# A decoder block's last loop: a weight tile loaded earlier, a residual read before the end, and 56 blocks of u spread over 128 turns

## The chip, the cores and the metric

One core of a Trainium2 chip runs the whole kernel. The metric is device time in microseconds (us); lower is better. TensorE (PE) multiplies matrices, VectorE (DVE) and ScalarE (ACT) work elementwise, GpSimd (POOL) issues the indirect loads, and SyncE (SP) issues the other loads and stores. Each engine works through its instructions in a fixed order and waits at the first one whose inputs are not there.

## What is computed

The reference is one decoder layer on 512 tokens of width 1024. Two token mixers (a gated recurrence and a dilated window attention) come first, then a channel mixer that retrieves experts:

```
x = x + merged @ w_out
h2 = rms_norm(x)
x = x + peer_ffn(h2, peer_wq, peer_subkeys, peer_u, peer_v)

# peer_ffn: 16384 experts (128 x 128 keys), 8 heads, the best 16 of each head
hid = einsum('thkd,td->thk', u[ib], xb)
a   = gelu(hid) * gate
out = einsum('thk,thkd->td', a, v[ib])
```

All is float32. The change is in the last part, the product with v.

## The kernel before

The 512 tokens are four tiles of 128. For three of the tiles (`VD`) the kernel does not gather rows of v: it goes through all 16384 experts in 128 blocks of 128 and multiplies densely, with weights that are zero where a token did not choose an expert. For the fourth tile (T = 3) it gathers the chosen rows one index at a time; the first product is dense for two tiles and gathered for the other two.

Before the last loop, 72 blocks of u (`NPRE`) are multiplied with the tokens: `hidden(b)` (L794 to L812) loads one 512 KB block `ub` through SP (L804), and PE writes `ph` (L811), of which ScalarE makes `pre[b]` (L812). Each token's expert weights are meanwhile scattered into a table `g_d` in device memory (L704).

The last loop (L844 to L867) makes 128 turns, one block of v each:

- Every eighth turn (`GB` = 8) the next eight blocks' weights are loaded from `g_d` into `Gc` through SP (L849), 1536 KB. Two buffers take turns, in the pools `vs` and `dp`. The eight blocks of group 0 are already on chip.
- VectorE multiplies block b's weights with `pre[b]` in place (L852), and the result is split into a high and a low part, `ah` by ScalarE and `al` by VectorE (L853, in the helper at L96 and L97).
- SP loads the block of v, `vb` (L855, 512 KB, three buffers), and ScalarE and VectorE split it into `vh` (L857) and `vl` (L859), two buffers each.
- PE adds 18 products to six accumulators, two for each of the three tiles (L863): `ah` with `vh`, `ah` with `vl`, `al` with `vh`. The accumulators stay in PSUM for the whole loop.
- In the first 56 turns `hidden(b + 72)` (L866) makes the remaining blocks of u, here with both operands split (`uh`, `ul`, one buffer each; 24 products). Its result is stored where `pre[b]` lay.
- `rows(ROWS_D)` (L867) emits the gathered rows of tile 3: GpSimd loads 128 rows of u or v by index (L636) into one of four buffers (three `rowx`, one `row`), and VectorE multiplies or accumulates them (L648, L667). A `Pump` (class at L708) pays out 1.9 of them a turn. A row's load also waits for that turn's `vh` (L640).

Behind the loop the rest of the rows is emitted (L868), and each of the three tiles is finished (L869 to L875): the residual, which an earlier part wrote to the output, is read back into the one buffer `row`, the two accumulators are added, and the tile is written.

The order in which the code emits the instructions is only a priority. A planner simulates the engines and queues when the kernel is built, and sets each engine's order by what is ready then in the simulation. So a step may run some turns after the turn that emits it.

Of the kernel before, what the change touches and what calls it, by code (L numbers as in the profile page):

```python
# [8 lines left out]
F32 = mybir.dt.float32  # L9
# [9 lines left out]
P = 128  # L19
S = 512  # L20
D = 1024
# [6 lines left out]
NKEY = 128  # L28
# [13 lines left out]
VD = (1, 2, 0)  # L42
NU = len(UD) * P
GT = 16
NGT = len(VD) * P // GT
GB = 8
# [5 lines left out]
NPRE, RING = 72, 56  # L52
# [3 lines left out]
GS = 4  # L56
ACTW = (4, 12)

ROWS_H, ROWS_D = 0.6, 1.9
UBUFS = 3  # L60
UK, WBUFS, WSBUFS, ATB = 4, 2, 4, 2

# [9 lines left out]
def kernel(ctx: ExitStack, tc: tile.TileContext, x, wst, par, cst, cols, g2, keys, u, v, ut, vr, out):  # L72
    nc = tc.nc
# [21 lines left out]
    def halves(hi, lo, x, eng=None):  # L95
        nc.scalar.activation(hi, x, AF.Copy)  # L96
        (eng or nc.vector).tensor_tensor(out=lo, in0=x, in1=hi.bitcast(F32), op=ALU.subtract)  # L97
        return hi, lo

    def accumulate(out, ws, xs, cut, w_stays, k0=0, last=KC - 1):  # L100

        for k, w in enumerate(ws, k0):
            if isinstance(w, tuple):
                x = xs[0][:, k], xs[1][:, k]
                ops = [(w[0], x[0]), (w[0], x[1]), (w[1], x[0])]
            else:
                ops = [(w, xs[:, k])]
            for i, (w, x) in enumerate(ops):
                l, r = (w[:, cut], x) if w_stays else (x[:, cut], w)
                nc.tensor.matmul(out, l, r, start=(k == 0 and i == 0), stop=(k == last and i == len(ops) - 1))  # L110
# [565 lines left out]
    g_d = dram.tile([P, NGT, NKEY, GT], F32, name="g_d")  # L676
# [52 lines left out]
    rows, scat = Pump(), Pump()  # L729
# [29 lines left out]
    gat = ctx.enter_context(tc.tile_pool(name="gat", bufs=1, side="left", **TILE))  # L759
# [26 lines left out]
    dp = ctx.enter_context(tc.tile_pool(name="dp", bufs=1, side="right", **TILE))  # L786
    rx = ctx.enter_context(tc.tile_pool(name="rx", bufs=3, side="right", **TILE))
    us = ctx.enter_context(tc.tile_pool(name="us", bufs=UBUFS, side="right", **TILE))
    row_places[:] = [(rx, "rowx")] * 3 + [(gat, "row")]
    pre, pre4 = [], [None]  # L790

    Gcs = [dp.tile([P, NGT, GB, GT], F32, name="Gc")]

    def hidden(b, pool):  # L794
        if RING <= b < NPRE:

            if (b - RING) % 4 == 0:
                pre4[0] = rq_pool.tile([P, 4, NU], F32, name="rq") if b - RING < 12 else rq_pool.tile([P, 4, NU], F32, name="keys_sb", bufs=1)
            dst = pre4[0][:, (b - RING) % 4]
        else:  # L800
            dst = dp.tile([P, NU], F32, name="pre", bufs=RING)
        pre.append(dst)
        ub = us.tile([P, KC, P], F32, name="ub")
        nc.sync.dma_start(out=ub, in_=ut[b].rearrange("p (k i) -> p k i", k=KC))  # L804
        pt = pool.tile([P, NU], F32, name="ph")
        if b < NPRE:

            accumulate(pt, [ub[:, k] for k in range(KC)], h32, slice(None), True)
        else:
            ubs = halves(us.tile([P, KC, P], F32R, name="uh", bufs=1), us.tile([P, KC, P], F32R, name="ul", bufs=1), ub)  # L810
            accumulate(pt, [tuple(a[:, k] for a in ubs) for k in range(KC)], (hH, hL), slice(None), True)  # L811
        return nc.scalar.activation(dst, pt, AF.Gelu)  # L812
# [26 lines left out]
    ph = ctx.enter_context(tc.tile_pool(name="ph", bufs=1, space=PSUM, side="left", **TILE))  # L839
    vs = ctx.enter_context(tc.tile_pool(name="vs", bufs=2, side="left", **TILE))  # L840
    pacc = ctx.enter_context(tc.tile_pool(name="pacc", bufs=1, space=PSUM, side="right", **TILE))
    ngu = NU // GT
    acc = [[pacc.tile([P, 512], F32, name=f"acc{t}{c}") for c in range(2)] for t in range(len(VD))]
    for b in range(NKEY):  # L844
        if b % GB == 0:
            Gc = Gcs[0]
            if b:
                Gc = (vs if b // GB % 2 else dp).tile([P, NGT, GB, GT], F32, name="Gc", bufs=1)
                nc.sync.dma_start(out=Gc, in_=g_d[:, :, b:b + GB])  # L849
        a = pre[b]  # L850
        gsl = Gc[:, :, b % GB]
        nc.vector.tensor_mul(gsl[:, :ngu], a.rearrange("p (g t) -> p g t", t=GT), gsl[:, :ngu])  # L852
        aH, aL = halves(vs.tile([P, NGT, GT], F32R, name="ah"), vs.tile([P, NGT, GT], F32R, name="al"), gsl)  # L853
        vb = vs.tile([P, D], F32, name="vb", bufs=3)
        nc.sync.dma_start(out=vb, in_=vr[b])  # L855
        vH = vs.tile([P, D], F32R, name="vh")
        behind[:] = [nc.scalar.activation(vH, vb, AF.Copy)]  # L857
        vL = vs.tile([P, D], F32R, name="vl")
        nc.vector.tensor_tensor(out=vL, in0=vb, in1=vH.bitcast(F32), op=ALU.subtract)  # L859
        for t in range(len(VD)):  # L860
            for i, (l, r) in enumerate([(aH, vH), (aH, vL), (aL, vH)]):
                for c in range(2):
                    nc.tensor.matmul(acc[t][c], l.rearrange("p g t -> p (g t)")[:, t * P:(t + 1) * P], r[:, c * 512:(c + 1) * 512],  # L863
                                     start=(b == 0 and i == 0), stop=(b == NKEY - 1 and i == 2))
        if b + NPRE < NKEY:
            hidden(b + NPRE, ph)  # L866
        rows(ROWS_D)  # L867
    rows(2 * S)  # L868
    for t, T in enumerate(VD):  # L869
        x1r = gat.tile([P, D], F32, name="row")  # L870
        nc.sync.dma_start(out=x1r, in_=out[T * P:(T + 1) * P])
        for c in range(2):
            cs = slice(c * 512, (c + 1) * 512)
            nc.vector.tensor_add(x1r[:, cs], acc[t][c], x1r[:, cs])
        nc.sync.dma_start(out=out[T * P:(T + 1) * P], in_=x1r)  # L875


def layout(inputs):
# [36 lines left out]
def build(arrays):  # L915
    import concourse.bacc as bacc
    nc = bacc.Bacc("TRN2", target_bir_lowering=False, num_devices=1)
    args = {k: nc.dram_tensor(f"in_{k}_dram", a.shape, mybir.dt.from_np(a.dtype), kind="ExternalInput").ap()
            for k, a in arrays.items()}
    out = nc.dram_tensor("out_0_dram", (S, D), F32, kind="ExternalOutput").ap()  # L920
    with tile.TileContext(nc, schedule_with_timeline_sim=True) as tc:
        kernel(tc, **args, out=out)
    return nc
# [8 lines left out]
```

## Time and profile before

| | us |
|---|---|
| median of three timed runs | 1810.34 (1808.81 to 1812.05) |
| the profiled execution, its own time | 1805.38 |
| its span in the trace | 1803.5 |
| start of the last loop's products in the span | 1059.3 |
| end of the last product | 1785.1 |

The rows below come from that one execution. A row of the timeline starts with the start in us from the span's start and the duration in us, then the engine, the line, the operation, what is written from what, and how many instructions are merged; in square brackets stands how long the engine was idle ahead of it and what ended that. "SPq" is SyncE's queue of issues. A row of a window gives the stretch, its length, each engine's busy time with its instructions, the clock that was granted to TensorE as a share of full speed, the busy share of the DMA engines and the GB/s moved. A row of the waits names who waited for whom, the total in us, how often, and the longest.

### The profile page before, as it was taken

The page shows a single profiled execution, that of the slowest core. Times are in us where ns is not written, and L with a number is a line of the kernel's source. Part 1 is how long each engine was busy: PE and PEld are TensorE (multiplying, and loading weights), DVE is VectorE, ACT ScalarE, POOL GpSimd, SP SyncE. Part 2 cuts the span into 40 slices and gives each one's busy share as a digit, 9 for nine tenths or more (in the row PEclk, how much of TensorE's full clock was granted, in tenths as well). Part 3 has the DMA queues.
Part 4 walks back from the last instruction along what each step waited for, and adds up shares of the span by engine and source line. Part 5 has one row for each costly group of instructions (what it writes and reads, how often), then busy time and mean ns, then how long its engine had stood idle before and what let it go on. Part 6 is the DMA issues. An engine that isn't in the chain of part 4 may idle for free.

```text
span 1803.5 us, 26810 instructions
## 1 busy us (share of the span) xinstructions
PE 1639.0 (91%) x9725; PEld 1450.2 (80%) x9725; DVE 1346.3 (75%) x2805; ACT 700.8 (39%) x1283; POOL 641.5 (36%) x502
## 2 busy tenths in 40 slices
PE   8998979789988799999899889999999999988995
PEld 7887968689877797888789877888888888867774
DVE  3113999989886669998985577787788887777774
ACT  3323434334344544523454553334344333323331
POOL 0000355766550004452442123334444444443330
PEclk9999979999989899999999999999999999989998
DMA  8776468788884336665667688999999998888885
GB/s 287 245 232 221 143 206 312 245 296 306 304 287 170 119 121 240 208 201 193 211 227 252 225 293 308 331 355 333 331 335 342 331 331 315 286 281 300 299 293 183
DMA packets 173380, 473.41 MB, mean 262 GB/s; under 512 B 14784, under 2 KB 62144, under 8 KB 173248
## 3 DMA queue, kind: packets, MB, share of 16 engines
q1 hardware_dynamic: 115840, 268.47, 43.9%
q0 software_dynamic: 55296, 201.35, 31.3%
q10 hardware_dynamic: 2112, 1.88, 0.3%
q8 instruction: 77, 1.26, 0.3%
q14 instruction: 55, 0.45, 0.1%
HBM read 442.80 MB, written 27.79 MB: 261 GB/s over the span
## 4 chain that ended last, share of the span: by engine, by line
PE 47%; DVE 25%; DMA 21%; issue 4%; ACT 2%; POOL 1%; DVEq 0%; POOLq 0%; ACTq 0%; SPq 0%
PE acc L863 18%; PE pp L110 16%; DMA Gc<-g_d 9%; PE ph L110 9%; DMA w<-in_wst_dram 2%; DMA rq<-in_u_dram,idx 2%; DVE e L687 2%; DVE rowx L648 2%; PE pg L701 2%; DMA rowx<-in_u_dram,idx 2%; DVE rq L648 1%; DVE row L648 1%; DVE eg L696 1%; DMA row<-in_u_dram,idx 1%; DVE wl L97 1%
## 5 line engine op out<-in xcount | busy, mean ns | idle before, releaser
L110 PE MATMUL ph<-h,ub 128*128 128x256 f32 x1152 | 265.4, 386 | 0.0
L863 PE MATMUL acc<-vl,ah 128*128 128x512 f32 x768 | 243.5, 398 | 18.0 <-DVE vl L859 18.0
L863 PE MATMUL acc<-vh,al 128*128 128x512 f32 x768 | 244.3, 396 | 0.0
L110 PEld LDWEIGHTS ph<-h,ub 128*128 128x128 f32 x1152 | 219.2, 195 | 29.8 <-issue 0.2
L863 PE MATMUL acc<-vh,ah 128*128 128x512 f32 x768 | 221.1, 396 | 9.8 <-ACT vh L857 9.8
L636 POOL DMA_INDIRECT rowx<-in_u_dram,idx x96 | 122.7, 1278 | 216.1 <-ACT pre L812 56.8
L636 POOL DMA_INDIRECT rowx<-in_v_dram,idx x96 | 130.7, 1362 | 193.2 <-DVE h2g L667 90.2
L863 PEld LDWEIGHTS acc<-vl,ah 128*128 128x128 f32 x768 | 145.2, 192 | 49.3 <-DVE vl L859 20.8
L863 PEld LDWEIGHTS acc<-vh,ah 128*128 128x128 f32 x768 | 143.9, 191 | 38.8 <-ACT vh L857 11.1
L863 PEld LDWEIGHTS acc<-vh,al 128*128 128x128 f32 x768 | 146.5, 192 | 30.5
L96 ACT ACTIVATE ah<-Gc 128x384 fp32r<-128x384 f32 x128 | 67.0, 524 | 264.0 <-PE acc L863 261.3
L859 DVE TENSOR_TENSOR vl<-vb,vh 128x1024 fp32r<-128x1024 f32 x128 | 156.1, 1219 | 11.6 <-ACT vh L857 11.2
L857 ACT ACTIVATE vh<-vb 128x1024 fp32r<-128x1024 f32 x128 | 135.6, 1060 | 45.3 <-DMA vb<-in_vr_dram 44.5
L636 POOL DMA_INDIRECT rq<-in_u_dram,idx x96 | 120.0, 1250 | 93.5 <-DVE rq L648 52.9
L648 DVE SCALAR_TENSOR_TENSOR rowx<-rowx,h2g 128x1024 f32<-128x1024 f32 x96 | 122.4, 1276 | 39.2 <-DMA rowx<-in_u_dram,idx 39.1
L648 DVE SCALAR_TENSOR_TENSOR rq<-rq,h2g 128x1024 f32<-128x1024 f32 x96 | 132.8, 1385 | 19.8 <-DMA rq<-in_u_dram,idx 19.6
L96 ACT ACTIVATE wh<-w 128x512 fp32r<-128x512 f32 x144 | 89.1, 629 | 128.8 <-PE pp L110 71.1
L110 PE MATMUL ph<-hH,ul 128*128 128x256 f32 x448 | 127.6, 285 | 5.1 <-DVE ul L97 5.1
L110 PE MATMUL ph<-hH,uh 128*128 128x256 f32 x448 | 127.8, 285 | 3.8 <-ACT pre L812 3.8
L667 DVE SCALAR_TENSOR_TENSOR h2g<-rowx,hid,h2g 128x1024 f32<-128x1024 f32 x95 | 121.7, 1281 | 8.4 <-DMA rowx<-in_v_dram,idx 8.0
L110 PE MATMUL ph<-hL,uh 128*128 128x256 f32 x448 | 127.7, 285 | 0.0
L701 PE MATMUL pg<-eg,e 128*128 128x128 f32 x768 | 104.5, 290 | 23.5 <-DVE eg L696 17.3
(289 smaller groups left out, 3611.9 us busy)
## 6 DMA issues: line engine op xcount, KB each, us to landing
ub<-in_ut_dram SPq DMA_DIRECT2D x128, 512.0 KB, 4.7
vb<-in_vr_dram SPq DMA_DIRECT2D x128, 512.0 KB, 7.1
w<-in_wst_dram SPq DMA_DIRECT2D x107, 512.0 KB, 5.2
g_d<-Gx SPq DMA_DIRECT2D x24, 960.0 KB, 4.6
Gc<-g_d SPq DMA_DIRECT2D x15, 1536.0 KB, 16.5
wh<-in_wst_dram SPq DMA_DIRECT2D x37, 256.0 KB, 4.9
wl<-in_wst_dram SPq DMA_DIRECT2D x33, 256.0 KB, 5.4
pairB<-in_x_dram SPq DMA_DIRECT2D x5, 512.0 KB
```

The lines of the kernel that those rows point to most:

```text
L96: nc.scalar.activation(hi, x, AF.Copy)
L97: (eng or nc.vector).tensor_tensor(out=lo, in0=x, in1=hi.bitcast(F32), op=ALU.subtract)
L110: nc.tensor.matmul(out, l, r, start=(k == 0 and i == 0), stop=(k == last and i == len(ops) - 1))
L636: d = nc.gpsimd.indirect_dma_start(out=r, out_offset=None, in_=src, in_offset=bass.IndirectOffsetOnAxis(ap=index, axis=0))
L648: nc.vector.scalar_tensor_tensor(r, r, 1.0, h2g[T], op0=ALU.mult, op1=ALU.mult, accum_out=hid[:, g, j:j + 1])
L667: nc.vector.scalar_tensor_tensor(acc, r, hid[:, g, j:j + 1], acc, op0=ALU.mult, op1=ALU.add)
L687: nc.vector.tensor_tensor(out=e1, in0=iota[:, None, :, 0].to_broadcast(by_token), in1=pk[:, ti, 0, tk, None].to_broadcast(by_token), op=AL ...
L696: nc.vector.tensor_tensor(out=eg, in0=e2.rearrange("p k q -> p q k"), in1=pkw[:, ti, tk, None].to_broadcast(by_token), op=ALU.mult)
L701: nc.tensor.matmul(pt[:, q], e1[:, q0 + q], eg[:, q0 + q], start=True, stop=True)
L857: behind[:] = [nc.scalar.activation(vH, vb, AF.Copy)]
L859: nc.vector.tensor_tensor(out=vL, in0=vb, in1=vH.bitcast(F32), op=ALU.subtract)
L863: nc.tensor.matmul(acc[t][c], l.rearrange("p g t -> p (g t)")[:, t * P:(t + 1) * P], r[:, c * 512:(c + 1) * 512], start=(b == 0 and i == 0 ...
```

## The change

- The weights `Gc` of group g + 1 are loaded in the middle of group g (turn 8g + 4), into the same two buffers.
- The 56 remaining blocks of u are emitted one in every 2.14 turns, the last by turn 118 (`ULAST` = 120), in place of one a turn in the first 56 turns.
- The gathered rows are emitted at 1.75 a turn in place of 1.9; what might be left is emitted in turn 123 (`XLAST`) and no longer behind the loop.
- In turn 123 the three tiles' residuals are read into the three `rowx` buffers. Behind the loop only the adds and the writes are left, and each tile is written in two halves.

```diff
--- before.py
+++ after.py
@@ -56,7 +56,9 @@
 GS = 4
 ACTW = (4, 12)
 
-ROWS_H, ROWS_D = 0.6, 1.9
+ROWS_H, ROWS_D = 0.6, 1.75
+
+ULAST, XLAST = 120, 123
 UBUFS = 3
 UK, WBUFS, WSBUFS, ATB = 4, 2, 4, 2
 
@@ -842,11 +844,12 @@
     ngu = NU // GT
     acc = [[pacc.tile([P, 512], F32, name=f"acc{t}{c}") for c in range(2)] for t in range(len(VD))]
     for b in range(NKEY):
-        if b % GB == 0:
-            Gc = Gcs[0]
-            if b:
-                Gc = (vs if b // GB % 2 else dp).tile([P, NGT, GB, GT], F32, name="Gc", bufs=1)
-                nc.sync.dma_start(out=Gc, in_=g_d[:, :, b:b + GB])
+        if b % GB == GB // 2 and b + GB < NKEY:
+
+            g = b // GB + 1
+            Gcs.append((vs if g % 2 else dp).tile([P, NGT, GB, GT], F32, name="Gc", bufs=1))
+            nc.sync.dma_start(out=Gcs[g], in_=g_d[:, :, g * GB:(g + 1) * GB])
+        Gc = Gcs[b // GB]
         a = pre[b]
         gsl = Gc[:, :, b % GB]
         nc.vector.tensor_mul(gsl[:, :ngu], a.rearrange("p (g t) -> p g t", t=GT), gsl[:, :ngu])
@@ -862,17 +865,22 @@
                 for c in range(2):
                     nc.tensor.matmul(acc[t][c], l.rearrange("p g t -> p (g t)")[:, t * P:(t + 1) * P], r[:, c * 512:(c + 1) * 512],
                                      start=(b == 0 and i == 0), stop=(b == NKEY - 1 and i == 2))
-        if b + NPRE < NKEY:
-            hidden(b + NPRE, ph)
+
+        if len(pre) < NKEY and (len(pre) - NPRE) * ULAST <= b * (NKEY - NPRE):
+            hidden(len(pre), ph)
         rows(ROWS_D)
-    rows(2 * S)
+        if b == XLAST:
+
+            rows(2 * S)
+            x1s = []
+            for T in VD:
+                x1s.append(rx.tile([P, D], F32, name="rowx"))
+                nc.sync.dma_start(out=x1s[-1], in_=out[T * P:(T + 1) * P])
     for t, T in enumerate(VD):
-        x1r = gat.tile([P, D], F32, name="row")
-        nc.sync.dma_start(out=x1r, in_=out[T * P:(T + 1) * P])
         for c in range(2):
             cs = slice(c * 512, (c + 1) * 512)
-            nc.vector.tensor_add(x1r[:, cs], acc[t][c], x1r[:, cs])
-        nc.sync.dma_start(out=out[T * P:(T + 1) * P], in_=x1r)
+            nc.vector.tensor_add(x1s[t][:, cs], acc[t][c], x1s[t][:, cs])
+            nc.sync.dma_start(out=out[T * P:(T + 1) * P, cs], in_=x1s[t][:, cs])
 
 
 def layout(inputs):
```

## Rows read from the trace of the kernel before

**Rows 1.** The page, part 1: busy us (share of the span) x instructions, by engine.
```profile
PE 1639.0 (91%) x9725; PEld 1450.2 (80%) x9725; DVE 1346.3 (75%) x2805; ACT 700.8 (39%) x1283; POOL 641.5 (36%) x502
```

**Rows 2.** Windows: length, busy of PE, PEld, DVE, ACT, POOL, clock, DMA, GB/s.
```profile
1059.32:1580.54 521.22, 510.40 (x2822) 443.94 (x2821) 414.24 (x551) 200.07 (x279) 215.15 (x155) 0.99 0.92 327
1580.54:1785.08 204.54, 182.89 (x758) 147.86 (x756) 153.07 (x175) 60.96 (x81) 71.57 (x55) 0.93 0.81 282
...
1360.00:1485.00 125.00, 125.00 (x699) 109.30 (x699) 104.94 (x112) 50.01 (x70) 55.50 (x40) 1.00 0.95 337
```

**Rows 3.** Waits of PE in the loop: total us, times, longest us.
```profile
PE acc L863 <- DVE vl L859: 18.0, 6, 8.2
PE acc L863 <- ACT vh L857: 9.8, 3, 4.0
PE ph L110 <- DVE ul L97: 4.6, 5, 2.5
```

**Rows 4.** Timeline of PE: two turns' starts; a block of u, start and next.
```profile
1768.60 1.52 PE L863 MATMUL acc<-vh,ah 128*128 128x512 f32 x6
...
1772.68 1.52 PE L863 MATMUL acc<-vh,ah 128*128 128x512 f32 x6
...
1577.70 0.28 PE L110 MATMUL ph<-hH,uh 128*128 128x256 f32 x1
...
1580.54 0.63 PE L863 MATMUL acc<-vh,ah 128*128 128x512 f32 x2
```

**Rows 5.** Timeline of SP's queue: loads behind the cut.
```profile
1580.69 0.53 SPq L849 DMA_DIRECT2D Gc<-g_d  x1
1581.83 41.44 SPq L855 DMA_DIRECT2D vb<-in_vr_dram  x8
...
1706.59 61.48 SPq L855 DMA_DIRECT2D vb<-in_vr_dram  x14
```

**Rows 6.** Timeline, all engines: waits at Gc loads behind the cut.
```profile
1596.93 2.77 DVE L852 TENSOR_TENSOR Gc<-pre,Gc 128x256 f32<-128x256 f32 x8 [8.87 <-DMA Gc<-g_d]
1598.26 1.06 ACT L857 ACTIVATE vh<-vb 128x1024 fp32r<-128x1024 f32 x1 [5.17 <-DMA vb<-in_vr_dram]
...
1602.55 1.22 PE L863 MATMUL acc<-vl,ah 128*128 128x512 f32 x2 [8.20 <-DVE vl L859]
...
1643.49 1.66 PE L863 MATMUL acc<-vh,ah 128*128 128x512 f32 x6 [2.53 <-ACT vh L857]
...
1722.71 1.06 ACT L857 ACTIVATE vh<-vb 128x1024 fp32r<-128x1024 f32 x1 [6.16 <-DMA vb<-in_vr_dram]
...
1723.82 2.38 PE L863 MATMUL acc<-vh,ah 128*128 128x512 f32 x6 [3.29 <-ACT vh L857]
```

**Rows 7.** Waits of ScalarE, 1059 to 1585 us, then 1585 to 1785 us.
```profile
ACT vh L857 <- DMA vb<-in_vr_dram: 20.1, 9, 4.1
...
ACT vh L857 <- DMA vb<-in_vr_dram: 23.6, 4, 6.9
```

**Rows 8.** Timeline behind the last product: SP's issues and VectorE's adds.
```profile
1787.26 0.33 SPq L871 DMA_DIRECT2D row<-out_dram  x1
1790.94 1.29 DVE L874 TENSOR_TENSOR row<-acc,row 128x512 f32<-128x512 f32 x2 [6.34 <-DMA row<-out_dram]
...
1798.42 1.29 DVE L874 TENSOR_TENSOR row<-acc,row 128x512 f32<-128x512 f32 x2 [6.19 <-DMA row<-out_dram]
1799.73 0.34 SPq L875 DMA_DIRECT2D out_dram<-row  x1
```

**Rows 9.** Row loads, L636: POOL in windows; then forms, ns, first and last start.
```profile
1050.00:1785.00 735.00, 289.57 (x212) 0.97 0.89 315
1360.00:1485.00 125.00, 55.50 (x40) 1.00 0.95 337
...
L636 POOL DMA_INDIRECT rowx<-in_u_dram,idx x63: 933/1307/1999, 1055.9 to 1330.0; - x63
L636 POOL DMA_INDIRECT row<-in_v_dram,idx x32: 932/1336/2855, 1342.0 to 1763.3; - x32
...
DMA to landing us min/median/max: 4.8/7.6/13.7
```

## The prediction

> **What bounds the kernel now.** I read the page first: TensorE (PE) is busy 91% of the span, VectorE 75% [rows 1]. A share that high hides where the rest is lost, so next I cut the last loop of 128 turns at the place where the last u block is through. The loop's first product stands at 1059.3 us, its last ends at 1785.1. Up to 1580.5 PE is busy 510.4 of 521.2 us at a granted clock of 0.99 with the DMA engines at 0.92; after that 182.9 of 204.5 us at 0.93, DMA at 0.81 [rows 2]. The same loop is tight while u blocks run beside the v blocks, and loose once they are used up.
>
> How many turns lie behind the cut: after the Gc load at 1580.69 SP issues four runs of vb loads, of 8, 8, 8 and 14 (the first and the last are shown) [rows 5], 38 in all, so the first of them is block 90; three blocks are held ahead, and the turn that starts at 1580.54 is number 86. Thus 86 turns and all 56 u blocks lie before the cut and 42 turns behind it.
>
> What they need when nothing is late: turns follow each other every 4.08 us (1768.60, 1772.68), and a u block takes PE from 1577.70 to 1580.54, 2.84 us [rows 4]. Before the cut 86 x 4.08 + 56 x 2.84 = 509.9 us are needed and 521.2 taken: 11.3 lost, 2.2%. Behind it 42 x 4.08 = 171.4 are needed and 204.5 taken: 33.2 lost, 8.3 for each of the four Gc loads there. The whole loop needs 681.3 us and takes 725.8, so 44.5 us are to be had, three quarters of it in the last third. PE's own list of waits puts 32.4 us on three lines: 18.0 on vl, 9.8 on vh, 4.6 on ul [rows 3]; the other 12 are products at the lower clock behind the gaps (a granted clock of 0.93 behind the cut is 2.4 GHz for most of the time and 1.2 for the rest).
>
> Why it waits is seen at one load. Gc is issued at 1580.69 [rows 5]. VectorE stands 8.87 us until it lands, then multiplies eight blocks; only behind these, on the same in-order engine, comes vl, and PE stands 8.20 us. The vb load issued right behind Gc, at 1581.83, is late too: ScalarE waits 5.17 us for it [rows 6]. So each boundary has two causes, Gc in front of VectorE and Gc in front of a vb.
>
> **The tail.** After the last product three tiles are finished one after the other through one buffer: read back (1787.26), add (1790.94), write, read back, add (1798.42), last write issued at 1799.73 [rows 8]. From 1785.1 to the span's end are 18.4 us, with nothing on PE. The chain is 1059.3 + 725.8 + 18.4 = 1803.5; 1.9 us lie outside the span, own time 1805.4. The median of the three timed runs is 1810.3, 4.9 above; I work on the own time and add 4.9 at the end.
>
> **The change, part by part.** *Tail.* The three reads move to turn 123, into the three rowx buffers, so nothing is read back after the sums. Each accumulator is added as soon as it is ready. The last turn's products go tile by tile, 6 x 0.227 = 1.36 us each, and two adds take 1.29 [rows 8], so two tiles' adds lie beside PE and one pair is left. Then the last issue and what followed it: 1803.5 - 1799.73 = 3.8. New tail 0.2 + 1.3 + 3.8 = 5.3, saved 13.1 us. Six writes replace three; five of them are issued before the last and hidden. The reads are covered while the rows' buffers come free before the loop ends; the cover's loss is rival B. On SP's queue the reads stand ahead of the vb loads of turns 124 to 127, which would wait with them.
>
> *Gc half a turn of the group early.* The same 15 loads, at turns 4, 12 to 116. Their buffer was last read four turns before, so SP does not wait at the new place. VectorE's wait goes: four turns are at least 16.3 us, and in the u stretch 21.7, where 16.2 are needed from issue (1580.69) to landing (1596.93). What is late next is the vb behind Gc. ScalarE's waits for vb are 20.1 us before the cut (11 loads, 1.8 each) and 23.6 us behind it (4 loads, 5.9 each) [rows 7]; a turn with its share of u takes 5.93 us before the cut and 4.08 behind it. With the new spread it takes 4.08 + 2.84 x 56/118 = 5.43 for all loads. Along the line between these two points the wait is 2.9 us per load. PE feels only what is above about 2.9 (ScalarE waited 6.16 us at the last load [rows 6], PE 3.29 right after it [rows 6]), so about 0 reaches PE. Bounds: 0 per load, and 1.2 if the wait is the 4.1 that was the longest before the cut [rows 7]; 0 to 18 us for 15 loads. I take 4, near the lower end, because the nearer rows are those with u.
>
> *u over the whole loop.* The same 56 blocks at one per 2.14 turns instead of one per 1.54; each moves with its load on SP, two splits and 24 products. Nothing is added. It lays DMA and PE work evenly: the stretch 1360 to 1485 is the best evidence that this mix can run, as PE is busy all 125.0 us of it with DMA at 0.95 [rows 2], and it holds more u per turn than the new loop (18 T + 24 U = 699 products and 4.08 T + 2.84 U = 125.0 us give 21.7 turns with 12.9 blocks of u, 0.59 a turn against 56/118 = 0.47). A u block is emitted nine turns before its last use at the latest, so a wait for it is taken as 0; if it is late, it sits in front of VectorE like Gc now.
>
> *Rows 1.75 instead of 1.9 a turn.* 212 rows are loaded in the loop [rows 9]; at 1.75 they are all emitted by turn 122. No operation more or less; taken as 0, its risk is rival B.
>
> *What else may be late* (rows landing late, splits queued on VectorE): from 0 to the whole 11.3 us lost before the cut today, scaled to the loop, 2.2% of 681 = 15. Some of that is Gc's, which goes; I take 8.
>
> **Sum.** Loop 681.3 + 4 + 8 = 693; tail 5.3. 1059.3 + 693.3 + 5.3 + 1.9 = 1759.8, 45.6 us less than 1805.4, and with the 4.9 the forecast is **1765 us** (-2.5%). Its own range: 1753 with nothing lost, 1786 with 18 + 15.
>
> **Rivals.** *B: the rows end last.* The loop's 212 row loads are issued from 1055.9 to 1763.3, 0.30 a us; 40 in the tight 125 us, 0.32 [rows 9]. The new loop asks 1.75/5.43 = 0.32, as fast as the best stretch. At 0.30 the last row is issued at 1763, after PE's new end; its landing 7.6 us later [rows 9], its multiply-add 1.3, the read that needs its buffer 3.7 (from 1787.26 to the add at 1790.94 [rows 8]), and an add and a write as in the tail, 5.1, give a span of 1781: **1788 us**. For it: today the last row is issued in turn 122, though at 1.9 a turn the code emits it in turn 112. Against: the mean of 0.30 has the Gc stalls in it, and 0.32 ran where PE was full.
>
> *C: the wait moves from Gc to the vb behind it.* It decides from a cost of (725.8 + 13.1 - 681.3)/15 = 3.8 us a load: above that the kernel is slower than before, and at the 8.3 of the loose stretch it is 681.3 + 124 = 806 of loop, **1877 us**. For it: the vb issued 1.1 us behind Gc fed vh at 1598.26, 1.3 us after VectorE had its Gc [rows 6]. The Trainium skill, "DMA: Bandwidth & Descriptors", section "Queues, rings and completion order", says descriptors on a queue's rings are consumed in ring order, so that an earlier issue of Gc would only push the vb loads of mid-group back; the trace agrees with the order here (1596.93, then 1598.26), not with the price. Against: with u in the turns, PE's three waits for vh, 9.8 us [rows 3], all stand in the loose part, the first at 1643.49, the last at 1723.82 [rows 6].
>
> *D: the order on the engines does not follow the code.* A planner places the work; today u blocks emitted over 56 turns run over 86. If Gc and u end up where they are, only the tail is won: 1805.4 - 13.1 + 4.9 = **1797 us**.
>
> **How the numbers follow.** Forecast 0.56, B 0.22, D 0.11, C 0.11, of which 0.04 near its point of balance and 0.07 above it. A difference of 0.2% (3.6 us) is about what can be told from no change. Faster 0.89 (forecast, B, D), same 0.04, slower 0.07. The range goes from 1750 (no loss in the loop, own time 3 us nearer to the median) to 1797, which takes in B and D; C is left out.
>
> **What would show it.** Right: no wait of VectorE for Gc; PE above 97% and clock at 0.99 in every stretch of the loop; u blocks up to about turn 118; no read of the output after the last product, and 5 us from there to the end. Wrong: ScalarE waiting over 4 us for vb at each load and PE for vh (C); rows still landing after the last product (B); two stretches of different tightness again (D); PE waiting for a u block's product after turn 118.

## The result, and the profile after

The changed kernel takes 1786.08 us (median; 1781.29 to 1791.66), 24 us less than before: ratio 0.9883, 95% interval 0.9851 to 0.9915. Its profiled execution took 1782.34 us, with a span of 1780.6. The forecast was 45 us less.

The page's first part, and windows of the last loop: whole, then in three stretches. Columns as in [rows 1] and [rows 2].

```profile
PE 1637.9 (92%) x9725; PEld 1449.5 (81%) x9725; DVE 1343.1 (75%) x2805; ACT 702.0 (39%) x1283; POOL 663.1 (37%) x502
```

```profile
1067.41:1773.07 705.66, 686.83 (x3578) 586.29 (x3576) 564.08 (x725) 261.97 (x360) 310.33 (x211) 0.99 0.92 325
...
1067.41:1300.00 232.59, 224.64 (x1158) 191.70 (x1157) 182.23 (x281) 86.27 (x118) 90.03 (x69) 0.99 0.94 329
1300.00:1550.00 250.00, 245.94 (x1304) 211.39 (x1303) 201.83 (x247) 95.31 (x133) 117.62 (x77) 0.99 0.92 330
1550.00:1760.00 210.00, 204.30 (x1071) 174.33 (x1071) 171.19 (x190) 78.69 (x108) 102.69 (x67) 1.00 0.91 321
```

The loose last third is gone: PE is busy 97%, 98% and 97% of the three stretches (224.64/232.59 and so on), where [rows 2] has 98% and 89%, and the granted clock is 0.99 to 1.00 in each, where [rows 2] has 0.93 behind the cut. The loop went from 725.8 to 705.7 us, the tail from 18.4 to 7.5 (1780.6 - 1773.1). But the loop does not reach the 681.3 that PE needs.

The waits in the loop (who waited for whom, total us, times, longest), as [rows 3] and [rows 7]. First VectorE's wait for Gc in the kernel before, then the changed kernel:

```profile
DVE Gc L852 <- DMA Gc<-g_d: 86.9, 15, 8.9
```

```profile
DVE Gc L855 <- DMA Gc<-g_d: 69.0, 15, 7.2
ACT vh L860 <- DMA vb<-in_vr_dram: 50.9, 19, 6.6
...
PE acc L866 <- DVE vl L862: 10.3, 9, 2.7
PE ph L112 <- DVE ul L99: 5.4, 6, 2.2
PE acc L866 <- ACT vh L860: 3.6, 2, 3.0
```

VectorE still waits at all 15 Gc loads, which the prediction said would go. One load in the timeline of all engines (start, us; in brackets the idle time ahead and what ended it), as [rows 6]; the next of vl follows a later load:

```profile
1102.13 0.53 SPq L851 DMA_DIRECT2D Gc<-g_d  x1
...
1119.48 2.77 DVE L855 TENSOR_TENSOR Gc<-pre,Gc 128x256 f32<-128x256 f32 x8 [4.73 <-DMA Gc<-g_d]
1120.78 1.06 ACT L860 ACTIVATE vh<-vb 128x1024 fp32r<-128x1024 f32 x1 [6.62 <-DMA vb<-in_vr_dram]
1121.88 2.40 PE L866 MATMUL acc<-vh,ah 128*128 128x512 f32 x6 [3.01 <-ACT vh L860]
...
1436.24 0.96 PE L866 MATMUL acc<-vl,ah 128*128 128x512 f32 x2 [2.70 <-DVE vl L862]
```

It is the picture of [rows 6] with smaller gaps: VectorE 4.73 us at this Gc in place of 8.87 (over all 15 loads 69.0 us in place of 86.9), PE at most about 3 in place of 8.20. What follows asks why the wait is there at all, and which part of the change made the gaps small.

### The profile page after: what moved, and what is told of

It reads as the page before. It is cut to its first block, busy times and chain, and to the rows that moved or that the text cites. A ratio compares the mean times of both kernels' runs of the same rounds, so it can differ in the third digit from the quotient of the medians.

```text
span 1780.6 us, 26815 instructions
## 1 busy us (share of the span) xinstructions
PE 1637.9 (92%) x9725; PEld 1449.5 (81%) x9725; DVE 1343.1 (75%) x2805; ACT 702.0 (39%) x1283; POOL 663.1 (37%) x502
## 4 chain that ended last, share of the span: by engine, by line
PE 39%; DVE 29%; DMA 23%; issue 5%; ACT 2%; POOL 2%; DVEq 0%; SPq 0%; POOLq 0%; ACTq 0%
PE pp L112 15%; PE acc L866 13%; DMA Gc<-g_d 7%; PE ph L112 7%; DMA w<-in_wst_dram 4%; DMA row<-in_u_dram,idx 2%; DVE e L689 2%; DVE h2g L669 2%; DVE rowx L650 2%; DMA rowx<-in_v_dram,idx 2%; DMA vb<-in_vr_dram 2%; DVE rq L650 2%; PE pg L703 1%; DVE wl L99 1%; DVE eg L698 1%
## 5 line engine op out<-in xcount | busy, mean ns | idle before, releaser
L866 PE MATMUL acc<-vh,al 128*128 128x512 f32 x768 | 239.9, 394 | 0.0
L638 POOL DMA_INDIRECT rowx<-in_v_dram,idx x96 | 154.4, 1608 | 153.1 <-DVE h2g L669 62.4
L866 PEld LDWEIGHTS acc<-vh,ah 128*128 128x128 f32 x768 | 139.9, 188 | 29.7 <-ACT vh L860 4.0
L860 ACT ACTIVATE vh<-vb 128x1024 fp32r<-128x1024 f32 x128 | 135.9, 1062 | 53.9 <-DMA vb<-in_vr_dram 50.9
L669 DVE SCALAR_TENSOR_TENSOR h2g<-rowx,hid,h2g 128x1024 f32<-128x1024 f32 x95 | 121.6, 1280 | 19.8 <-DMA rowx<-in_v_dram,idx 19.7
```

The costliest lines, as they stand in the source:

```text
L638: d = nc.gpsimd.indirect_dma_start(out=r, out_offset=None, in_=src, in_offset=bass.IndirectOffsetOnAxis(ap=index, axis=0))
L669: nc.vector.scalar_tensor_tensor(acc, r, hid[:, g, j:j + 1], acc, op0=ALU.mult, op1=ALU.add)
```

## The experiments

Each time is followed by its ratio to the kernel before, which was run beside it, with a 95% interval. Loop lengths, tails and waits are those of one profiled execution of each kernel.

**The parts alone.** Two kernels move only the Gc load: into the kernel before, and back out of the changed one.

```
# gc_only: the kernel before with
-        if b % GB == 0:
...
+        if b % GB == GB // 2 and b + GB < NKEY:
+            g = b // GB + 1
...
+            nc.sync.dma_start(out=Gcs[g], in_=g_d[:, :, g * GB:(g + 1) * GB])
# gc_old_place: the changed kernel with these lines the other way round
```

> The kernel before with only the first part of the change: the Gc load written half a group earlier in the code. Theory 1 (the planner had already put the load there, because it issues a load as soon as its buffer is free): every engine's order stays as it was, so 1810 us within 0.2%, and VectorE still waits about 87 us for Gc in 15 waits. Rival (the load now stands half a group earlier on SP and VectorE's wait goes): PE loses the 18 us on vl and some of the 12 us at the low clock, 1785 to 1795 us. As the order is that of the kernel before, the run also tells how much the start of the last loop's first product (1059.3 us in the profile of before, 1067.4 in that of the changed kernel) moves by chance: if by chance, it may stand anywhere from 1055 to 1070 here.

> The changed kernel with the Gc load put back to the group's first turn. Theory 1: no difference, 1786 us within 0.3%, VectorE waits about 69 us for Gc in 15 waits, loop of about 706 us. Rival: without the early load the loop is 15 to 25 us longer, 1800 to 1810 us.

gc_only: 1807.36 us, ratio 0.9997 (0.9961 to 1.0032). gc_old_place: 1779.24, 0.984 (0.9808 to 0.9873). Waits of VectorE for Gc, and the loop's window, first of gc_only, then of gc_old_place:

```profile
DVE Gc L853 <- DMA Gc<-g_d: 82.9, 15, 9.7
```

```profile
1062.38:1782.66 720.28, 688.38 (x3578) 587.54 (x3576) 566.78 (x725) 261.16 (x360) 288.42 (x210) 0.98 0.90 317
```

```profile
DVE Gc L854 <- DMA Gc<-g_d: 63.0, 15, 6.9
```

```profile
1063.46:1768.56 705.10, 685.42 (x3578) 586.85 (x3576) 564.06 (x723) 261.98 (x360) 310.97 (x211) 0.99 0.91 324
```

The reason stands in the built kernels. The order of instructions on each of the five engines is the same in gc_only as in the kernel before, and the same in gc_old_place as in the changed kernel: **that part of the edit changes nothing**. The position in the code is only a priority, and the planner already issued each load when its buffer came free: in the changed kernel 14 of the 15 issues on SP stand 0.03 to 0.07 us behind the end of the split `al` that reads that buffer last, the one of block 7, 15, 23 and so on. In the kernel before and in the changed one alike, the loads for groups 1, 2, 3, 4, ... 15 stand on SP behind 3, 10, 18, 26, ... 114 vb loads. Where VectorE's list holds the eight multiplications of a group (changed kernel; splits are those of `al`, one a turn):

```
group   first block   its 8 multiplications stand behind split number
  2          16             11
  3          24             18
  4          32             26
  5          40             34
```

So VectorE does the eight in one bunch, five to six turns before the first is used. Why the planner puts them there was not looked at; presumably the load lands there in its simulation. On the chip the load lands later, and VectorE, in order, stands there with vl queued behind. The wait is for weights that nobody needs yet.

The two other parts alone:

```
# tail_only: the kernel before with the change's XLAST block and its end
# spread_only: the kernel before with
-        if b + NPRE < NKEY:
-            hidden(b + NPRE, ph)
+        if len(pre) < NKEY and (len(pre) - NPRE) * ULAST <= b * (NKEY - NPRE):
+            hidden(len(pre), ph)
```

> The kernel before with only the new end: residuals read in turn 123 into the rowx buffers, rows left over emitted there, halves written. Theory 1: last product to end of span 7.5 us instead of 18.4 as in the changed kernel, loop as before at 726 us: 1799 us. Rival (the rows end last and hold back the reads): 12 us or more from the last product to the end, 1804 us or slower.

> The kernel before with only the u blocks spread (1.9 rows a turn, old end, old Gc place). Theory 1: loop of 706 us as in the changed kernel (20 us shorter), end of 18.4 us: 1790 us; together with the end alone this makes up the whole of the change's 24 us and more. Rival (the spread gives little and the early Gc load gave the loop's gain): 1803 us or slower.

tail_only: 1798.19, 0.9937 (0.9894 to 0.9981). spread_only: 1804.08, 0.9969 (0.9916 to 1.0022), not to be told from the kernel before and 14 us above what was expected, though its loop is shorter. Windows of the loop and timeline of the end, tail_only, then spread_only:

```profile
1065.67:1780.28 714.61, 688.44 (x3578) 587.68 (x3576) 569.21 (x727) 261.09 (x360) 283.41 (x210) 0.99 0.90 321
```

```profile
1778.29 3.68 DVE L880 TENSOR_TENSOR rowx<-acc,rowx 128x512 f32<-128x512 f32 x6 [2.67 <-PE acc L865]
```

```profile
1070.94:1780.27 709.33, 687.25 (x3578) 586.79 (x3576) 562.08 (x723) 262.04 (x360) 329.19 (x210) 0.99 0.90 320
```

```profile
1778.63 1.22 DVE L673 TENSOR_TENSOR row<-h2g,row 128x1024 f32<-128x1024 f32 x1 [2.74 <-DMA row<-out_dram]
1782.52 0.33 SPq L874 DMA_DIRECT2D row<-out_dram  x1
...
1802.29 0.34 SPq L878 DMA_DIRECT2D out_dram<-row  x1
```

The tail of tail_only is 5.1 us (span 1785.4), near the prediction's 5.3; 7.5 was expected of this run. In spread_only tile 3's sum (1778.63) now ends with the loop and uses the buffer `row`; the three tiles queue behind it through that same buffer, and the tail grows to 25.8 us (span 1806.1). The spread pays for itself only with the new end. The fourth part, rows at 1.75 a turn in place of 1.9, was not tried alone. The loops show no effect of it (709.3 us in spread_only at 1.9, 705.1 to 711.5 in three kernels at 1.75); the tail is taken up below.

**The suspected wait, taken away in two ways.** First, each multiplication is held back on VectorE behind the split of the block two before it, so the bunch is gone and the loads stay as they are (`als` keeps the splits `al`, which are written out in the loop for that):

```
+        with (tc.issue_after(als[b - LAG].ins) if b >= LAG else ExitStack()):     # LAG = 2
             nc.vector.tensor_mul(gsl[:, :ngu], a.rearrange("p (g t) -> p g t", t=GT), gsl[:, :ngu])
```

> The changed kernel, with the multiplication of block b's weights held on VectorE behind the split of block b - 2 (an order, no new wait). Today the planner puts eight multiplications on VectorE some six turns ahead of their use, right where its simulation has the Gc load land, and VectorE stands 63 to 69 us behind them. Theory 2 (this bunch makes PE wait): VectorE's wait for Gc falls below 5 us, PE's waits in the loop from 19 to 22 us to under 8, loop of 690 to 695 us against 706, 1768 us. Rival A (the vb loads queued behind the 1536 KB of Gc make PE wait): VectorE's wait goes but vh still waits 40 to 50 us for vb and PE as before: loop of 702 to 708 us, 1778 to 1786 us. Rival B (the loop is bound by the DMA engines, which are busy 0.91 to 0.92): loop unchanged at 705 us whatever VectorE does.

1755.52 us, 0.9723 (0.9671 to 0.9776). Its loop's window, and the waits of ScalarE and PE:

```profile
1066.88:1747.31 680.43, 679.16 (x3580) 583.24 (x3579) 565.44 (x728) 257.68 (x360) 300.65 (x210) 1.00 0.94 336
```

```profile
ACT vh L864 <- DMA vb<-in_vr_dram: 50.7, 17, 5.8
...
PE acc L870 <- DVE vl L866: 1.1, 3, 0.5
```

VectorE has no wait for Gc left, and the loop takes what PE needs: 680.4 us, forecast need 681.3, and less than the 690 to 695 expected of this run. ScalarE still waits 50.7 us for vb behind the Gc loads, but all of PE's waits in the loop come to 1.1 us.

Second, the transfer is cut: four loads of 384 KB, each held behind one of four vb loads, with the multiplications left to the planner.

```
+        vload = nc.sync.dma_start(out=vb, in_=vr[b])
+        if g < NKEY // GB and b % GB < 4:                      # g = b // GB + 1
...
+            q = slice(b % GB * NGT // 4, (b % GB + 1) * NGT // 4)
+            with tc.issue_after(vload.ins):
+                nc.sync.dma_start(out=Gcs[g][:, q], in_=g_d[:, q, g * GB:(g + 1) * GB])
```

> The changed kernel with each Gc load cut into four loads of 384 KB, one behind each of four vb loads on SP's queue; the eight multiplications stay bunched. Rival A (a vb behind Gc is late by Gc's whole time): vh's waits for vb fall from 41 to 52 us to under 15 and the loop to 690 to 697 us, 1770 us. Theory 2 (the bunch on VectorE): VectorE waits longer than today, because the last quarter lands two turns later and the planner still places the eight multiplications where it believes the landing: 706 us or more of loop, 1780 to 1795 us.

> Both edits together: Gc in quarters between the vb loads and the multiplications held behind the split of two blocks before. Theory 2: as with the held multiplications alone, 1768 us within 3 us. Rival A: the best of the four, 1762 us, a further 5 to 8 us. Rival B (DMA bound): 1780 us.

gc_quarters: 1753.26, 0.9719 (0.9671 to 0.9767); late_quarters, both edits together: 1752.59, 0.9711 (0.9661 to 0.9762). Window and VectorE's wait in gc_quarters, with the time from issue to landing of a quarter:

```profile
1064.54:1743.07 678.53, 677.20 (x3578) 582.67 (x3576) 567.77 (x723) 262.42 (x360) 270.51 (x211) 1.00 0.95 337
```

```profile
DVE Gc L850 <- DMA Gc<-g_d: 6.1, 5, 2.0
```

```profile
DMA to landing us min/median/max: 3.2/10.8/13.9
```

That the quarters would make VectorE's wait longer, because the last is issued later, was a miss, and the loop is shorter than either expectation. In the built order the bunch stands a turn later in about half of the groups, and a quarter lands in a median of 10.8 us where a whole load of the kernel before takes 16.5, so most are there before VectorE comes to them. ScalarE's wait for vb falls to 1.4 us as well. The two cures bring the loop to the same floor (678.5, 680.4, and 676.8 together). mul_late reaches it with ScalarE's wait for vb left as it was, so what the changed kernel's loop loses by is VectorE's wait at the bunch, and not vb behind Gc.

With no Gc load at all (every turn uses group 0's weights, so the output is another):

> The changed kernel without the 15 Gc loads: all turns use the weights of the first group, so the wrong experts are weighted (the work on the engines stays). It takes away VectorE's wait, the delay of vb and 23.6 MB of small packets. It bounds what all three causes cost together. Theory 2 and rival A: loop of 685 to 690 us, 1762 us; rival B: 690 us or less with the DMA share falling from 0.92 to about 0.85. If the loop stays near 700 us, the cause of the loss is none of the three (rows landing late, PE's own pace).

1762.19 us, 0.9765 (0.9718 to 0.9813), slower than the three kernels with the cures, which do load Gc:

```profile
1066.62:1753.30 686.68, 679.76 (x3581) 582.26 (x3579) 564.51 (x725) 262.53 (x360) 280.08 (x210) 1.00 0.85 300
```

```profile
DVE h2g L669 <- DMA rowx<-in_v_dram,idx: 54.1, 41, 3.0
```

The planner puts the gathered rows some four turns earlier here (the last multiply-add stands behind split 123 of `al`, in the changed kernel behind 127), and VectorE waits 54.1 us for them. As a price of Gc this run is spoilt by that. It does show that taking the loads away altogether, with the DMA share at 0.85 against 0.95, does not by itself give a loop shorter than that of the two cures.

**The cures without the spread.** Does the spread matter once the bunch is gone? The same two edits on the kernel before:

> The kernel before with one edit: each block's multiplication on VectorE is held behind the split of two blocks before. u blocks, rows and end as before. Theory 2 (VectorE's bunch is the larger cause also here, the vb behind Gc the smaller, and only where turns are 4.08 us): VectorE's wait for Gc below 5 us, PE's waits for vl nearly gone, but its waits for vh of about 10 us stay in the stretch without u; loop of 692 to 700 us against 715 to 726, tail 18 to 19, 1780 us. Rival (the spread of u is what makes the loop whole): PE's waits shift but stay above 20 us, 1795 us or more. Second rival (the spread does nothing at all once the bunch is gone): loop of 680 to 684 us, 1768 us.

> The kernel before with Gc loaded in four quarters between the vb loads; the rest as before. In the changed kernel this alone made the loop 678.5 us, as both VectorE's wait (63 to 6 us) and vh's wait for vb (41 to 2 us) went. Theory 2: both causes go here too, so the loop comes near what PE needs, 682 to 690 us, though u stays in the first 86 turns; 1772 us. Rival (without the spread the stretch without u stays loose because rows and loads crowd the first stretch): 700 us of loop or more, 1785 us.

before_late: 1786.73, 0.9871 (0.9838 to 0.9905), loop 704.0. before_quarters: 1781.18, 0.9842 (0.9813 to 0.9871), loop 692.9. Both loops are longer than expected (692 to 700 and 682 to 690). In before_quarters the quarters do not clear the bunch as they do with the spread:

```profile
DVE Gc L848 <- DMA Gc<-g_d: 39.3, 12, 6.0
```

PE's waits in before_late, and two of its stretches, with u blocks and behind the last of them:

```profile
PE acc L867 <- ACT vh L861: 16.8, 5, 6.6
PE acc L867 <- DVE vl L863: 2.0, 1, 2.0
```

```profile
1300.00:1560.00 260.00, 260.00 (x1461) 227.69 (x1461) 213.50 (x249) 103.19 (x145) 100.00 (x79) 1.00 0.95 337
1600.00:1765.00 165.00, 151.34 (x637) 123.55 (x636) 128.55 (x153) 50.81 (x69) 68.32 (x46) 0.95 0.83 288
```

Without the bunch the stretch with u is full to the last microsecond, and the stretch without u is still loose: 151.34 of 165 us, from vb behind Gc. Of PE's 16.8 us of waits for `vh`, 13.4 (1.8, 5.0 and 6.6) stand behind the last u block, which ends at 1564 us, and 3.4 at the first two loads of the loop. Loop lengths side by side, us (mean where there are several kernels; the lower row has one profile each, with Gc in whole loads):

| | u in the first 56 turns | u spread |
|---|---|---|
| bunch | 720.2 (725.8, 720.3, 714.6) | 707.9 (705.7, 705.1, 709.3, 711.5) |
| bunch held back | 704.0 | 680.4 |

The spread is worth 12 us with the bunch and 24 without it, the bunch 16 us without the spread and 27 with it. Each hides part of what the other costs. The upper row shows how far single profiles scatter: 11 us between kernels whose loops differ in nothing but the last turns.

**The end.** Is the tail longer than forecast because the residuals are read late into the rows' buffers? In end_ub they go into the buffers of the u blocks (`ub`, and `uh` for tile 3), which are free by then in the changed kernel's order; best is late_quarters with that end; best_rows and best_rows21 emit the rows at 1.9 and 2.1 a turn.

```
-                x1s.append(rx.tile([P, D], F32, name="rowx"))
+                x1s.append(us.tile([P, KC, P], F32, name="ub").rearrange("p k i -> p (k i)"))
-        x1r = gat.tile([P, D], F32, name="row")          # tile 3
+        x1r = late_pool[0].tile([P, KC, P], F32, name="uh", bufs=1).rearrange("p k i -> p (k i)")
```

> The changed kernel with the three residuals read into the buffers of ub, and that of tile 3 into the buffer of uh, all free after the last u block, instead of the buffers of the gathered rows. Theory 3 (the end is 7.5 to 9.8 us instead of 5.3 because the read for tile 3 waits for the last row's buffer and its add stands on VectorE ahead of the six adds of the accumulators): no read of the output within the last 15 us, 4.5 to 6 us from the last product to the end, 2 to 3 us less than the changed kernel. Rival (the last rows themselves set the end): 7.5 us or more as now.

> Quarters of Gc, held multiplications and the residuals in the buffers of ub and uh, on the changed kernel. Theory 2 and 3: loop of 677 to 681 us, end 4.5 to 6.5 us, 1749 us, below every kernel so far.

> The kernel with quarters of Gc, held multiplications and residuals in other buffers, with the rows at 1.9 a turn instead of 1.75: on VectorE the last row now stands ahead of the last turn's split, three turns earlier. Theory 3b (the last rows' multiply-adds, queued among and ahead of the six adds, make the end 7.6 to 7.8 us instead of 5.3): 5 to 5.8 us from the last product to the end, loop still 677 to 680 us, 1750 us. Rival (six half writes and their landing make the end): 7.5 us or more as now.

> The same at 2.1 rows a turn: the last row stands eight turns ahead of the end on VectorE. Theory 3b: end of 5 to 5.8 us as at 1.9; the denser rows in the last turns may cost PE up to 5 us of the loop if VectorE or the DMA engines have no room: 677 to 683 us, 1750 to 1755 us. Rival: end 7.5 us or more.

end_ub: 1782.11, 0.9833 (0.9796 to 0.9871), tail 7.6 against 7.5: taking the reads away gains nothing here. From late_quarters to best the same edit takes the tail from 9.8 to 7.8, still not to the 4.5 to 6.5 expected. best: 1753.05, 0.9687 (0.9662 to 0.9713). Its VectorE at the end:

```profile
1739.83 3.92 DVE L669 SCALAR_TENSOR_TENSOR h2g<-rowx,hid,h2g 128x1024 f32<-128x1024 f32 x3
1743.71 1.29 DVE L889 TENSOR_TENSOR ub<-acc,ub 128x512 f32<-128x512 f32 x2
1744.91 1.28 DVE L669 SCALAR_TENSOR_TENSOR h2g<-row,hid,h2g 128x1024 f32<-128x1024 f32 x1
1746.11 2.48 DVE L889 TENSOR_TENSOR ub<-acc,ub 128x512 f32<-128x512 f32 x4
...
1748.50 1.22 DVE L673 TENSOR_TENSOR uh<-h2g,uh 128x1024 f32<-128x1024 f32 x1
```

It never stands still: the last rows' multiply-adds (L669) share the end with the six adds, so the rows end last by a little. Emitting them sooner should help. It gives a tail of about 6.1 us in both kernels (5 to 5.8 was expected), but 1777.53 (0.9831, 0.98 to 0.9863) at 1.9 and 1803.94 (0.9979, 0.9962 to 0.9996) at 2.1. PE's wait in best_rows, with the write that ends it, and then in best_rows21:

```profile
PE ph L112 <- ACT uh L98: 21.3, 1, 21.3
```

```profile
1744.91 0.34 SPq L674 DMA_DIRECT2D out_dram<-uh  x1
```

```profile
PE ph L112 <- ACT uh L98: 43.9, 1, 43.9
```

Tile 3's sum now comes before the last u blocks, takes the one buffer `uh`, and holds it until it is written; the last u blocks' split waits for that, and PE with it. That is my own choice of buffer, not a fault of the change. PE's stop also gives VectorE time to finish the rows, so these two tails are no clean test; no_gc, whose rows end four turns earlier, has 5.1 us like tail_only. The best that were run are gc_quarters, late_quarters and best, all about 1753 us, 3% under the kernel before.

## Why the prediction was wrong

On the profiled execution the sum was 1759.8 and the time 1782.3. The 22.5 us: start +8.1, loop +12.4, tail +2.2, and 0.2 less outside the span.

- **What bounds the kernel: right.** The loop's need of 681.3 us was derived from two turns and one u block; three kernels come to 680.4, 678.5 and 676.8 once the waits are gone. PE is the floor.
- **The Gc step failed.** It said: issued four turns early, the load lands in time, and VectorE's wait goes. The wait stayed at all 15 loads, 69.0 us for 86.9, and that edit changed no engine's order: with the load back in its old place the wait is 63.0 (gc_old_place). Both facts were within reach. The section on the kernel before says that code order is only a priority. And the working itself counted the turn at 1580.54 as number 86: a load issued at 1580.69 [rows 5] in turn 86 cannot be the one for the group that begins at turn 88, which had its buffer long before; it was for group 12, blocks 96 to 103, ten turns off. VectorE waited 8.87 us at 1596.93 [rows 6] for weights that are used some seven turns later. Read so, the row says that the place of the multiplication is at fault, not the time of the load. The Trainium skill, "DMA: Bandwidth & Descriptors", section "Rules for kernel authors", says to issue a DMA early, compute, and wait late. mul_late agrees: waiting late alone, with the loads where they were, took the loop from 705.7 to 680.4 us; the issue moved early in the code alone (gc_only) gave no measurable change.
- **The bound that should have held it.** The 8 us for "splits queued on VectorE" covers this mechanism but was sized as a leftover. What stands in its place is the 24.4 us between 705.7 and 681.3, 25.2 by mul_late. The upper end of the forecast's own range, 1786, is near the result, but by another sum: it puts 18 us on vb behind Gc. The stated range, 1750 to 1797, was opened that far for B and D. That the result lies in it is luck and no sign that the sum was right.
- **vb behind Gc (rival C, and the 4 us): right in size.** ScalarE waits 50.9 us for vb, 3.4 for each of the 15 loads, where the line between the two stretches said 2.9. With u in most turns PE feels at most 1.1 us of it (mul_late); in the stretch without u it feels 13.4 (before_late). The point of decision was PE's slack in the turn, as argued.
- **The spread: right in kind.** By the table it gives 12 us as the kernel stands, and 24 without the bunch.
- **The engines' order does not follow the code (rival D): half true.** True for the Gc loads. Not for u: the last u split stands behind the 119th `al` split, as the spread wants.
- **The rows end last (rival B): in small.** The last row load is issued at 1758.0 us, 15 us before the end of the last product, not after it, but VectorE does tile 3's sum right ahead of the six adds.

The tail, 7.5 for 5.3, in the timeline of VectorE and SP of the changed kernel:

```profile
1767.17 0.33 SPq L672 DMA_DIRECT2D row<-out_dram  x1
...
1771.59 1.22 DVE L673 TENSOR_TENSOR row<-h2g,row 128x1024 f32<-128x1024 f32 x1 [2.84 <-DMA row<-out_dram]
1772.73 3.67 DVE L882 TENSOR_TENSOR rowx<-acc,rowx 128x512 f32<-128x512 f32 x6
```

The step had two of three pairs of adds beside PE. All six start at 1772.73, 0.3 us before the last product ends, because VectorE stood 2.84 us for tile 3's residual. In tail_only, where the rows end earlier, the six adds start at 1778.29, 2.0 us before the last product ends, and the tail is 5.1. Where the reads were moved away (end_ub, best), the last rows' multiply-adds took the place of that wait. So the likely cause of the 2.2 us is the rows at 1.75 a turn, which the prediction took as 0; the rate alone was not tried.

The start, +8.1, is not the change: ahead of the loop all five engines have the same order in both kernels. The loop's first product stands between 1059.3 and 1071.6 us in the 16 profiles of this study, 1066.4 on average, and the profile of before has the earliest. So the sum started from an early loop; the 4.9 us that were added between its own time and the median cover most of that.

Of the 24 us to the kernel before, then: about 12 from the spread (by the table's means), 11 from the new end with its rows at 1.75 (18.4 to 7.5), none from the Gc load.

## What to carry to other kernels

Where a planner orders the engines, first look whether an edit of the code's order changes any engine's list; the Gc edit changed none. For a wait at a load, ask when the waiting instruction's result is needed: if that is turns later, hold the instruction back, or make the load land sooner, but issuing it earlier in the code was not the lever here. A price read from one stretch holds for its mix: with the same 50 us of waits for vb, PE lost 1 us where u blocks ran nearly to the end, and 17 where they ended early, 13 of them behind the last one.

## What the runs showed of the hardware

A load's issue on SP can itself take long. A vb load's issue takes 0.33 us (median), but in the changed kernel the first one behind a Gc load of 1536 KB lasted 4.8 to 11.2 us at 14 of the 15 loads. At the longest, the u load behind it was issued only then:

```profile
1589.28 0.53 SPq L851 DMA_DIRECT2D Gc<-g_d  x1
1590.42 11.23 SPq L858 DMA_DIRECT2D vb<-in_vr_dram  x1
1601.75 0.39 SPq L806 DMA_DIRECT2D ub<-in_ut_dram  x1
```

With Gc in quarters the longest single issue of a vb is 2.4 us (gc_quarters), and with no Gc load at all 0.8 us (no_gc), so it goes with the large load. What SP stands for there the records do not name.

TensorE ran the whole loop at DMA shares of 0.94 and 0.95 with waits of 1.1 and 1.3 us in all (mul_late, gc_quarters), so the busy DMA engines were not a bound here.
